# Where three kinds of weight conversions and small loads stand in a two-layer decoder kernel: two slabs in a feature buffer, conversions in the norm chains, loads moved forward

## The chip, the core and the metric

The kernel runs on one core of one Trainium2 chip. The metric is device time in microseconds (us): the median of three runs of the kernel. One further execution was profiled. Its trace records each instruction of the core's engines: TensorE (PE, with its weight loads as PEld), VectorE (DVE), ScalarE (ACT), GpSimd (POOL) and SyncE (SP), which issues almost all of the transfers here. A name such as L235 is line 235 of the kernel before.

## The reference

Two layers over 256 tokens of width 1024, batch 1, all in float32. Each layer is a mixer of three attention groups and then a GeGLU feed-forward network (FFN) with a causal convolution of width 3:

```
for l in range(DEPTH):                       # DEPTH = 2, SEQ = 256, D_MODEL = 1024
    h = rms_norm(x, ln_mix_pre[l])
    x = x + rms_norm(hybrid_mixer(h, rel_bias, w_in[l], b_f[l], q_norm[l], kv_norm[l],
                                  w_uq[l], w_ukv[l], w_o[l]), ln_mix_post[l])
    h = rms_norm(x, ln_ffn_pre[l])
    x = x + rms_norm(conv_ffn(h, w_up[l], conv_w[l], conv_b[l], w_down[l]), ln_ffn_post[l])

def conv_ffn(h, w_up, conv_w, conv_b, w_down):   # D_FF = 2816
    u = h @ w_up                                 # 1024 x 5632
    u = causal_depthwise_conv3(u, conv_w) + conv_b
    g, val = split(u, 2)
    return (gelu(g) * val) @ w_down              # 2816 x 1024
```

The mixer begins with one projection `h @ w_in` (1024 x 2726) and ends with `merged @ w_o` (1024 x 1024). Its columns c (low-rank latents, normed with the gains `q_norm` and `kv_norm`) and v are projected first.

## The kernel before, in words

**Weights come in slabs.** Every weight matrix is read in pieces ("slabs") of up to 128 x 1024 float32. `plan()` lists them in the order of use. For one layer that is c, v, the other columns of `w_in`, o (8 slabs), and then the FFN: slabs gu, g and u of `w_up` and d0 to d21 of `w_down`. In the FFN, d(2i-2) and d(2i-1) follow the up slabs of block i.

**A slab passes through three steps.** `fetch()` issues its load on SP into a `raw` buffer `st` (5 of them, `RBUFS`). `hi_next()` copies it on ACT into a rounded half `wh` (L228). `lo_next()` subtracts that half from the original on DVE and gives `wl` (L235). A product of two float32 matrices is then made from three matmuls (`mm3`, `mm3s`: high by high, high by low, low by high), so PE needs `wh` for the first and `wl` for the second of them. The next fetch into a raw buffer waits for the subtraction that last read it.

**How far ahead a slab is converted.** `slab(key)` is called just before a matmul group. It calls `convert`, which converts up to `AHEAD` = 6 slabs past the one asked for, as long as fewer than `WBUFS` = 8 slabs are converted and not yet used up (`nxt - done < WBUFS`). While `hold` is set, only the slab asked for is made sure of, and the conversions are placed by hand. Each engine runs its instructions in the order in which the program issues them.

**The FFN's loop.** 11 blocks (`NI`) of 256 hidden columns. For i = 2 to 10, `up(i)` makes four accumulations of 128 columns (gate and value), each evicted by ACT (L850) and DVE (L851). `conv_glu(i)` runs the convolution, the gelu and the split on ACT (L863, L876, L275) and DVE (L871, L873, L880, L276). Then `down(i-1, t)` multiplies block i-1 into the accumulators `ac[t]` for the two halves t = 0, 1 of the tokens. The last block runs its two column halves one after the other, each with its own `conv_glu`. For the last four blocks (`SKEW` = 4) the product for t = 1 is put off ("late"). Their d slabs, d14 to d21, so stay in converted buffers until the end. After the loop come `down(7, 1)`, `down(10, 0)`, the post-norm of t = 0 and the pre-norm of t = 0 for the next layer, during which PE runs the late products for t = 1. Then come the same two norms for t = 1, while PE begins the next layer's c and v columns for t = 0.

**The norm chains.** `postnorm` and `prenorm` each take two squares on ACT (L291), a short reciprocal root on POOL (L296 to L298), and two or four DVE operations on 512 columns (L327 and L332, or L312). An argument `mid` is called inside the chain and places conversions there. `to_feat` transposes the normed tokens on PE (L319) and splits them (L275, L276) into a feature pair. A feature pair is one tile `xx` of 128 x 4096 in the pool `xtp`, which has 2 buffers: in the FFN one holds the FFN's input (`fh`, `fl`), the other held the mixer's merged output (`mh`, `ml`).

**The same at the border from mixer to FFN.** The products with `w_o` for t = 1 run while t = 0 is normed, and `up_nat` for t = 0 starts while t = 1 is normed. PE needs slab gu6 for the third step of `up_nat(1, 0)`, then the transposes of t = 1 (in its `mid`), then slab gu7.

**Small loads.** The tile `lc` holds `q_norm`, `kv_norm` and `b_f` of a layer (L605 to L607, 128, 64 and 3 KB). It is first read by the norm of the c columns (L427).

Of the kernel before, what the change touches and what calls it, by code (L numbers as in the profile page):

```python
# [10 lines left out]
F32 = mybir.dt.float32  # L11
F32R = mybir.dt.float32r
# [52 lines left out]
def kernel(ctx: ExitStack, tc: tile.TileContext, x, rel_bias, ln_mix_pre, ln_mix_post,  # L65
# [18 lines left out]
    def acc():  # L84
        return [wk(), wk()]
# [7 lines left out]
    def feat_pair():  # L93
        xx = xtp.tile([128, 8, 2, S], F32R, name="xx")
        return xx[:, :, 0, :], xx[:, :, 1, :]
# [105 lines left out]
    def shaped(t, shp):  # L201
        v = t[:, :int(np.prod(shp))]
        if len(shp) == 3:
            return v.rearrange("p (a g b) -> p a g b", g=shp[1], b=shp[2])
        return v if len(shp) == 1 else v.rearrange("p (a b) -> p a b", b=shp[-1])
# [12 lines left out]

    lows = []

    def hi_next():
        key, (_, shp) = slabs[nxt[0]]
        nxt[0] += 1
        n = int(np.prod(shp))
        st = staged.pop(0)
        h = wpool.tile([128, 1024], F32R, name="wh")
        lo = wpool.tile([128, 1024], F32R, name="wl")
        nc.scalar.activation(h[:, :n], st[:, :n], AF.Copy)  # L228
        lows.append((h, lo, st, n))
        loaded[key] = (shaped(h, shp), shaped(lo, shp))  # L230

    def lo_next():
        if lows:
            h, lo, st, n = lows.pop(0)
            nc.vector.tensor_tensor(lo[:, :n], st[:, :n], h[:, :n].bitcast(F32), op=ALU.subtract)  # L235

    def split_next():
        hi_next()
        lo_next()

    def split_last():
        hi_next()
        lo_next()
# [9 lines left out]
    def slab(key):  # L253
        i = index[key]
        convert(i if hold[0] else i + AHEAD)
        assert key in loaded, key
        left[i] -= 1
        done[0] += left[i] == 0
        return loaded[key]
# [115 lines left out]
    for l in range(L):  # L375
        lc = lay.tile([128, 390], F32, name="lc")
        if l == 0:
            xh, xl = feat_pair()
        else:
            xh, xl = nx  # L380
# [222 lines left out]

        def small_loads():
            nc.sync.dma_start(lc[:, :256], bcast(q_norm[l], 256))  # L605
            nc.sync.dma_start(lc[:, 256:384], bcast(kv_norm[l], 128))
            nc.sync.dma_start(lc[:, 384:390], bcast(b_f[l], 6))  # L607
# [23 lines left out]
        if l == 0:  # L631
# [7 lines left out]
            to_feat(1, hn[1], xh, xl)  # L639
            small_loads()  # L640
            nc.sync.dma_start(cst[:, C_R:], cst_d[:, 256 + C_R:])
# [14 lines left out]
        else:  # L656
            small_loads()
            hold[0] = False
# [136 lines left out]
        hi_next()  # L795
        postnorm(1, wacc[1], g_post, mid=split_last)
        lo_next()
        fetch()
        hn1 = prenorm(1, halves(g_fpre), mid=hi_next)
        lo_next()  # L800
        split_next()
        hold[0] = False
# [104 lines left out]
        for i in range(2, NI):  # L907
# [10 lines left out]
            if i == 2:  # L918
                ac.extend(acc() for _ in range(2))
            if i == 4:  # L920
                g_fpost = gain(ln_ffn_post[l])
# [11 lines left out]
        hold[0] = True  # L933
        postnorm(0, ac[0], g_fpost, out_v[0] if last else None)
        if not last:
            hn_next[0] = prenorm(0, halves(g_pre))
        down(late.pop(0), 1)
        for n in range(2):
            for j in late:
# [4 lines left out]
                down(j, 1, (n,))  # L944
        if not last:
            convert(index[(l + 1, "c", 3)])

        def two():
            fetch()
            if not last:  # L950
                hi_next()
                hi_next()
                lo_next()

        postnorm(1, ac[1], g_fpost, out_v[1] if last else None, mid=two)
        if not last:
            lo_next()
            hn_next[1] = prenorm(1, halves(g_pre), mid=two)
            lo_next()
# [28 lines left out]
```

## Time and profile before

| what | value |
|---|---|
| median of 3 runs | 646.12 us (645.0 to 646.38) |
| the profiled execution, its own time | 644.71 us |
| span of its trace, first to last instruction | 642.8 us |
| PE busy (matmuls) | 621.8 us, 97% of the span |
| PEld busy | 526.7 us, 82% |
| DVE busy | 475.9 us, 74% |
| ACT busy | 402.6 us, 63% |
| POOL busy | 31.7 us, 5% |
| HBM | 107.78 MB read, 169 GB/s over the span |

The table is to be read with the stages in mind: a share over the whole span says little of the few places at which PE stands still. In the rows further down, a time in brackets is how long the engine stood idle before the instruction, with what released it. Matmul ends are modelled, so the distance between two starts is the safer measure of what PE lost.

### The profile page before, as it was taken

The page shows a single profiled execution, that of the slowest core. Times are in us where ns is not written, and L with a number is a line of the kernel's source. Part 1 is how long each engine was busy: PE and PEld are TensorE (multiplying, and loading weights), DVE is VectorE, ACT ScalarE, POOL GpSimd, SP SyncE. Part 2 cuts the span into 40 slices and gives each one's busy share as a digit, 9 for nine tenths or more (in the row PEclk, how much of TensorE's full clock was granted, in tenths as well). Part 3 has the DMA queues.
Part 4 walks back from the last instruction along what each step waited for, and adds up shares of the span by engine and source line. Part 5 has one row for each costly group of instructions (what it writes and reads, how often), then busy time and mean ns, then how long its engine had stood idle before and what let it go on. Part 6 is the DMA issues. An engine that isn't in the chain of part 4 may idle for free.

```text
span 642.8 us, 9945 instructions
## 1 busy us (share of the span) xinstructions
PE 621.8 (97%) x3522; PEld 526.7 (82%) x3522; DVE 475.9 (74%) x963; ACT 402.6 (63%) x801; POOL 31.7 (5%) x74
## 2 busy tenths in 40 slices
PE   7999999999999999999899999999999999999996
PEld 3998988778888888887688988878788888888864
DVE  4683786576888887777777568757588888888873
ACT  5567556656667666665655766566575676666751
POOL 2210000120000000000031000002100000000001
PEclk9999999999999999999999999999999999999999
DMA  7885343346446675553545833433554666566401
GB/s 256 243 278 184 132 154 110 99 157 201 140 140 217 240 252 185 185 184 131 154 140 154 278 132 142 126 94 131 176 184 139 229 228 197 197 196 197 164 1 65
DMA packets 79653, 109.48 MB, mean 170 GB/s; under 512 B 4269, under 2 KB 69523, under 8 KB 79604
## 3 DMA queue, kind: packets, MB, share of 16 engines
q1 hardware_dynamic: 78018, 106.09, 50.5%
q10 hardware_dynamic: 1250, 1.87, 0.8%
q0 software_dynamic: 336, 0.90, 0.5%
q8 instruction: 27, 0.44, 0.3%
q14 instruction: 22, 0.18, 0.1%
HBM read 107.78 MB, written 1.06 MB: 169 GB/s over the span
## 4 chain that ended last, share of the span: by engine, by line
PE 86%; DVE 6%; ACT 3%; issue 2%; POOL 1%; DMA 0%; DVEq 0%; POOLq 0%; ACTq 0%
PE wk L845 19%; PE wk L847 10%; PE wk L262 8%; PE wk L263 8%; PE wk L264 8%; PE wk L269 7%; PE wk L272 7%; PE wk L270 7%; DVE wl L235 2%; PE wk L577 2%; PE wk L585 2%; PE wk L544 1%; PE wk L319 1%; PE wk L542 1%; ACT wh L228 1%
## 5 line engine op out<-in xcount | busy, mean ns | idle before, releaser
L235 DVE TENSOR_TENSOR wl<-st,wh 128x1024 fp32r<-128x1024 f32 (+3 forms) x200 | 230.2, 1184 | 71.1 <-ACT wh L228 70.7
L228 ACT ACTIVATE wh<-st 128x1024 fp32r<-128x1024 f32 (+3 forms) x200 | 196.3, 1022 | 23.0 <-DMA st<-in_w_in_dram 9.1
L845 PE MATMUL wk<-xx,wh 128*128 128x512 f32 x576 | 157.5, 395 | 1.5 <-ACT wh L228 1.5
L845 PEld LDWEIGHTS wk<-xx,wh 128*128 128x128 f32 x576 | 99.6, 189 | 16.1 <-ACT wh L228 1.9
L847 PEld LDWEIGHTS wk<-xx,wl 128*128 128x128 f32 x576 | 88.2, 189 | 12.9 <-DVE wl L235 1.0
L847 PE MATMUL wk<-xx,wl 128*128 128x256 f32 x576 | 91.8, 281 | 0.1
L263 PE MATMUL wk<-wl,hp 128*128 128x512 f32 x176 | 69.5, 395 | 3.0 <-DVE wl L235 3.0
L262 PE MATMUL wk<-wh,hp 128*128 128x512 f32 x176 | 68.9, 391 | 1.1 <-ACT wh L228 1.1
L264 PE MATMUL wk<-wh,hp 128*128 128x512 f32 x176 | 68.9, 392 | 0.0
L270 PE MATMUL wk<-wl,xx 128*128 128x512 f32 (+3 forms) x160 | 58.6, 366 | 3.6 <-DVE wl L235 3.6
L269 PE MATMUL wk<-wh,xx 128*128 128x512 f32 (+3 forms) x160 | 59.5, 372 | 0.6 <-ACT xx L275 0.3
L269 PE MATMUL wk<-xx,wh 128*128 128x256 f32 x192 | 49.5, 291 | 0.0
L270 PE MATMUL wk<-xx,wh 128*128 128x256 f32 x192 | 48.0, 283 | 0.0
L272 PE MATMUL wk<-wh,xx 128*128 128x512 f32 (+3 forms) x160 | 45.1, 363 | 0.9 <-DVE xx L276 0.9
L850 ACT ACTIVATE t<-wk 128x256 f32<-128x256 f32 x72 | 25.9, 372 | 28.8 <-PE wk L847 28.5
L863 ACT ACTIVATE t<-t,cv 128x256 f32<-128x256 f32 x72 | 38.6, 593 | 6.3 <-DVE t L851 6.0
L263 PEld LDWEIGHTS wk<-wl,hp 128*128 128x128 f32 x176 | 33.0, 188 | 11.5 <-DVE wl L235 5.2
L275 ACT ACTIVATE hp<-hv 128x256 fp32r<-128x256 f32 x44 | 18.4, 418 | 35.8 <-DVE hv L880 35.8
L262 PEld LDWEIGHTS wk<-wh,hp 128*128 128x128 f32 x176 | 33.1, 188 | 8.1 <-ACT wh L228 1.6
L264 PEld LDWEIGHTS wk<-wh,hp 128*128 128x128 f32 x176 | 33.1, 188 | 6.8
L269 PEld LDWEIGHTS wk<-xx,wh 128*128 128x128 f32 x192 | 36.7, 191 | 1.7 <-issue 1.3
L851 DVE TENSOR_TENSOR t<-wk,t 128x256 f32<-128x256 f32 x72 | 28.9, 420 | 11.5 <-ACT t L850 11.4
(158 smaller groups left out, 911.3 us busy)
## 6 DMA issues: line engine op xcount, KB each, us to landing
st<-in_w_up_dram SPq DMA_DIRECT2D x72, 512.0 KB, 5.1
st<-in_w_down_dram SPq DMA_DIRECT2D x44, 512.0 KB, 4.7
st<-in_w_in_dram SPq DMA_DIRECT2D x24, 512.0 KB, 4.7
st<-in_w_o_dram SPq DMA_DIRECT2D x16, 512.0 KB, 3.1
st<-in_w_up_dram SPq DMA_DIRECT2D x32, 256.0 KB, 2.9
st<-in_w_in_dram SPq DMA_DIRECT2D x8, 390.0 KB, 7.2
st<-in_w_in_dram SPq DMA_DIRECT2D x8, 384.0 KB, 3.1
st<-in_w_in_dram SPq DMA_DIRECT2D x5, 416.0 KB, 3.3
```

The costliest lines, as they stand in the source:

```text
L228: nc.scalar.activation(h[:, :n], st[:, :n], AF.Copy)
L235: nc.vector.tensor_tensor(lo[:, :n], st[:, :n], h[:, :n].bitcast(F32), op=ALU.subtract)
L262: nc.tensor.matmul(o, stat[0], mov[0], start=start, stop=False)
L263: nc.tensor.matmul(o, stat[0], mov[1], start=False, stop=False)
L264: nc.tensor.matmul(o, stat[1], mov[0], start=False, stop=stop)
L269: nc.tensor.matmul(o, stat[0], mov[0], start=start and i == 0, stop=False)
L270: nc.tensor.matmul(o, stat[0], mov[1], start=False, stop=False)
L272: nc.tensor.matmul(o, stat[1], mov[0], start=False, stop=stop and i == n - 1)
L845: nc.tensor.matmul(ps, wh[:, k % 4, c], both(fh, k), start=k == 0, stop=False)
L847: nc.tensor.matmul(ps[:, :S], wl[:, k % 4, c], fh[:, k, :], start=False, stop=k == 7)
L851: nc.vector.tensor_tensor(us[a][:, g, :], ps[:, :S], us[a][:, g, :], op=ALU.add)
L863: nc.scalar.activation(y[:, g, :], us[a][:, g, :], AF.Identity, scale=cv[:, 88 + cj:89 + cj], bias=cv[:, 132 + cj:133 + cj])
```

## The change

- At block 6 of each FFN, a third tile `ex` is taken from the pool of feature pairs. The converted halves of d14 and d15 (`2 * (NI - SKEW)` is 14) go into it, not into the pool of 8. These two slabs no longer count against `WBUFS`.
- `hi_room()` is a `hi_next()` that runs only where a buffer is free and a slab is left. It stands in both norm chains of t = 0 and in those of t = 1 at the FFN's end.
- The order of conversions at the FFN's end is changed: two to three halves stand in other places among the norms of t = 1, and the slab v3 is converted by the next layer's second `slab` call.
- At the border from mixer to FFN, slab gu6 is converted in the post-norm of t = 1 (its `wl` behind it and ahead of the pre-norm), gu7's `wh` in the pre-norm.
- The loads of `lc` for layer 1 are issued at block 6 of layer 0's FFN, not at the start of layer 1.

```diff
+    extra = {}
+    apart = set()
...
         st = staged.pop(0)
-        h = wpool.tile([128, 1024], F32R, name="wh")
-        lo = wpool.tile([128, 1024], F32R, name="wl")
+        if key in extra:
+            h, lo = extra.pop(key)
+            apart.add(key)
+            done[0] += 1
+        else:
+            h = wpool.tile([128, 1024], F32R, name="wh")
+            lo = wpool.tile([128, 1024], F32R, name="wl")
...
+    def hi_room():
+        if nxt[0] < len(slabs) and nxt[0] - done[0] < WBUFS:
+            hi_next()
...
-        done[0] += left[i] == 0
+        done[0] += left[i] == 0 and key not in apart
...
         else:
-            small_loads()
             hold[0] = False
...
-        postnorm(1, wacc[1], g_post, mid=split_last)
+
+        def three():
+            hi_next()
+            lo_next()
+            hi_next()
+
+        postnorm(1, wacc[1], g_post, mid=three)
+        lo_next()
         lo_next()
         fetch()
         hn1 = prenorm(1, halves(g_fpre), mid=hi_next)
         lo_next()
-        split_next()
         hold[0] = False
...
+            if i == 6:
+                ex = xtp.tile([128, 8, 2, S], F32R, name="xx").rearrange("p a b c -> p (a b c)")
+                for j in range(2):
+                    extra[(l, "d", 2 * (NI - SKEW) + j)] = [ex[:, 2048 * j + 1024 * n:2048 * j + 1024 * n + 1024]
+                                                            for n in range(2)]
+                if not last:
+                    lc = lay.tile([128, 390], F32, name="lc")
+                    small_loads(l + 1)
...
         hold[0] = True
-        postnorm(0, ac[0], g_fpost, out_v[0] if last else None)
+        fetch()
+        postnorm(0, ac[0], g_fpost, out_v[0] if last else None, mid=hi_room)
+        lo_next()
         if not last:
-            hn_next[0] = prenorm(0, halves(g_pre))
+            hn_next[0] = prenorm(0, halves(g_pre), mid=hi_room)
+            lo_next()
         down(late.pop(0), 1)
...
-        if not last:
-            convert(index[(l + 1, "c", 3)])
+        fetch()
+        hi_room()
+        lo_next()
+        hi_room()
 
         def two():
+            lo_next()
             fetch()
-            if not last:
-                hi_next()
-                hi_next()
-                lo_next()
+            hi_room()
+            hi_room()
 
         postnorm(1, ac[1], g_fpost, out_v[1] if last else None, mid=two)
         if not last:
             lo_next()
-            hn_next[1] = prenorm(1, halves(g_pre), mid=two)
+            lo_next()
+            hn_next[1] = prenorm(1, halves(g_pre), mid=hi_room)
             lo_next()
```

## Rows read from the trace of the kernel before

**Rows 1.** The page, part 1: busy us, share, instructions.

```profile
PE 621.8 (97%) x3522; PEld 526.7 (82%) x3522; DVE 475.9 (74%) x963; ACT 402.6 (63%) x801; POOL 31.7 (5%) x74
```

**Rows 2.** Windows: stretch, its length, busy us (instructions) by engine, granted clock, DMA.

```profile
125.00:150.00 25.00, 24.02 (x114) 19.58 (x113) 18.42 (x24) 15.42 (x26) 4.92 (x11) 1.00 0.47 151
...
278.23:292.20 13.97, 13.97 (x78) 12.07 (x77) 12.27 (x22) 9.69 (x18) 0.00 (x0) 1.00 0.48 162
...
325.00:345.00 20.00, 17.71 (x95) 15.81 (x94) 15.36 (x25) 12.16 (x26) 5.51 (x12) 1.00 0.54 153
...
638.00:640.00 2.00, 0.00 (x0) 0.00 (x0) 1.46 (x3) 0.00 (x0) 0.27 (x1) 1.00 0.03 11
640.00:642.80 2.80, 0.00 (x0) 0.00 (x0) 0.00 (x0) 0.00 (x0) 0.00 (x0) 0.74 0.48 179
```

**Rows 3.** Timeline of PE, mixer to FFN: start, us, instruction, [idle before <-releaser].

```profile
140.92 0.39 PE L269 MATMUL wk<-wh,xx 128*128 128x512 f32 x1
142.28 0.50 PE L270 MATMUL wk<-wl,xx 128*128 128x512 f32 x1 [0.98 <-DVE wl L235]
142.62 0.40 PE L269 MATMUL wk<-wh,xx 128*128 128x512 f32 x1
```

**Rows 4.** Timeline of PE, end of layer 0's FFN and start of layer 1.

```profile
295.90 0.64 PE L847 MATMUL wk<-xx,wl 128*128 128x256 f32 x4
297.31 1.21 PE L845 MATMUL wk<-xx,wh 128*128 128x512 f32 x4 [0.77 <-ACT wh L228]
...
313.52 0.49 PE L262 MATMUL wk<-wh,hp 128*128 128x512 f32 x1 [1.15 <-ACT wh L228]
...
315.12 0.39 PE L264 MATMUL wk<-wh,hp 128*128 128x512 f32 x1
...
323.53 1.03 PE L319 MATMUL wk<-ident,scr 128*128 128x128 f32 x8
...
339.69 0.64 PE L272 MATMUL wk<-wh,xx 128*128 128x416 f32 x2 [0.92 <-DVE xx L276]
```

**Rows 5.** Timeline of PE, end of layer 1's FFN.

```profile
610.18 1.19 PE L845 MATMUL wk<-xx,wh 128*128 128x512 f32 x4 [0.77 <-ACT wh L228]
...
626.58 0.40 PE L264 MATMUL wk<-wh,hp 128*128 128x512 f32 x1
```

**Rows 6.** Timeline of DVE, end of layer 0's FFN and start of layer 1.

```profile
283.33 2.36 DVE L235 TENSOR_TENSOR wl<-st,wh 128x1024 fp32r<-128x1024 f32 x2 [0.53 <-ACT wh L228]
...
290.54 0.48 DVE L871 SCALAR_TENSOR_TENSOR t<-t,cv,t 128x255 f32<-128x255 f32 x1
...
300.25 0.48 DVE L871 SCALAR_TENSOR_TENSOR t<-t,cv,t 128x255 f32<-128x255 f32 x1
...
307.88 0.42 DVE L851 TENSOR_TENSOR t<-wk,t 128x256 f32<-128x256 f32 x1
...
321.99 1.42 DVE L312 SCALAR_TENSOR_TENSOR scr<-x,r,gain 128x512 f32<-128x512 f32 x2 [1.91 <-POOL r L298]
...
338.95 1.28 DVE L276 TENSOR_TENSOR xx<-wk,xx 128x512 fp32r<-128x512 f32 x2
```

**Rows 7.** Timeline of ACT, end of layer 0's FFN.

```profile
295.89 0.42 ACT L275 ACTIVATE hp<-hv 128x256 fp32r<-128x256 f32 x1 [0.83 <-DVE hv L880]
...
303.06 1.04 ACT L228 ACTIVATE wh<-st 128x1024 fp32r<-128x1024 f32 x1
...
310.69 0.42 ACT L275 ACTIVATE hp<-hv 128x256 fp32r<-128x256 f32 x1 [0.96 <-DVE hv L880]
...
312.42 2.63 ACT L228 ACTIVATE wh<-st 128x1024 fp32r<-128x1024 f32 x3
```

**Rows 8.** Timeline of SP's queue (issues), and landing of slabs from 245 to 300 us.

```profile
284.58 0.37 SPq L216 DMA_DIRECT2D st<-in_w_up_dram  x1
...
332.74 0.46 SPq L605 DMA_DIRECT2D lc<-in_q_norm_dram  x1
...
DMA to landing us min/median/max: 3.3/5.1/5.6
```

More of the change, by code (lines that the diff above doesn't have):

```diff
@@ L237, in split_next @@
     def split_next():
-        hi_next()
-        lo_next()
-    def split_last():
         hi_next()
@@ L375 @@
     for l in range(L):
-        lc = lay.tile([128, 390], F32, name="lc")
         if l == 0:
+            lc = lay.tile([128, 390], F32, name="lc")
             xh, xl = feat_pair()
@@ L601, in heads, with small_loads @@
                                          [vtile("c", t, h) for t in range(2)], r))
-        def small_loads():
+        def small_loads(l):
             nc.sync.dma_start(lc[:, :256], bcast(q_norm[l], 256))
@@ L639 @@
             to_feat(1, hn[1], xh, xl)
-            small_loads()
+            small_loads(0)
             nc.sync.dma_start(cst[:, C_R:], cst_d[:, 256 + C_R:])
@@ L656 @@
         else:
-            small_loads()
             hold[0] = False
@@ L919 @@
                 ac.extend(acc() for _ in range(2))
+            if i == 6:
[4 more added lines that the diff above has]
+                if not last:
+                    lc = lay.tile([128, 390], F32, name="lc")
+                    small_loads(l + 1)
             if i == 4:
@@ L944 @@
                 down(j, 1, (n,))
-        if not last:
-            convert(index[(l + 1, "c", 3)])
+        fetch()
+        hi_room()
+        lo_next()
+        hi_room()
         def two():
+            lo_next()
             fetch()
-            if not last:
-                hi_next()
-                hi_next()
-                lo_next()
+            hi_room()
+            hi_room()
         postnorm(1, ac[1], g_fpost, out_v[1] if last else None, mid=two)
```

## The prediction, made before the changed kernel ran

> **What bounds the kernel now.** I read the shares of the page first. PE is busy 97% of the span [rows 1], so the change can only win back what PE loses in its gaps, some 20 us, of which the start and the last norm chain are not touched. The windows come next, to see where the gaps lie: 1.0 us between mixer and FFN and 2.3 us around the start of layer 1 [rows 2], and, by PE's timeline, the end of each FFN [rows 4, 5]. There the reader is to look at starts. A matmul of 512 columns follows the one before after 0.2275 us, a group of eight in `up` takes 1.40 us.
>
> - Mixer to FFN, once in each layer: from 140.92 to 142.62 PE starts two matmuls in 1.70 us, where 0.455 is regular. PE loses 1.24 us to the `wl` of gu6 (0.98 idle, the rest is the filling of the pipeline) [rows 3].
> - End of layer 0's FFN: the group after 295.90 should start 0.47 later, at 296.37, and starts at 297.31. From there to 315.12 lie five groups of `up` (7.0 us) and 29 matmuls (6.6), and it takes 17.81 [rows 4]. Lost: 0.94 + 4.21 = 5.15 us, to the `wh` and `wl` of u21, d18, d19 and d21, all of them conversions that came late.
> - End of layer 1's FFN: the same 13.6 us of work takes 626.58 - 610.18 = 16.40, so 2.8 + 0.94 = 3.7 us [rows 5]. It is less because no table load and no slab of a next layer stand there.
>
> **Why these conversions come late.** In blocks 7 to 9 the late d slabs stay in the pool of 8, so `convert` finds no room and issues u21 behind `conv_glu(9)`, d18 to d20 in block 10, and d21 behind `conv_glu(10)` and the table load. I counted `nxt - done` by hand through both programs. With d14 and d15 apart, the two lost places return: g20 to u21 are issued in the first six groups of `up(9)`, d18 and d19 behind `conv_glu(9)`, d20, d21 and c0 in block 10, c1 behind the table load. No conversion is then late for PE. These edits add no instruction, and the tile they use was last read by the products with `w_o`.
>
> **The queues, and what is late next.** ACT and DVE run in order, and a conversion issued earlier stands ahead of other work. In `up(9)` DVE is already busy 12.27 of 13.97 us [rows 2], since a block without its t = 1 product is shorter for PE and not for DVE. So I follow DVE from 283.33, where both programs are still alike. Two conversions take 2.36 us [rows 6], so they start 1.14 apart; an eviction (L851, 0.42) is taken as 0.34 apart.
>
> 1. DVE now has six conversions (d16, d17, g20, g21, u20, u21) and four evictions ahead of the convolution of block 9: 283.35 + 6 x 1.14 + 4 x 0.34 = 291.55. Before, it began at 290.54 [rows 6]. Lag 1.0.
> 2. The last `hp` of block 9 moves from 295.89 [rows 7] to 296.9. Then d18's `wh` runs to 298.3, DVE subtracts d18 and d19 to 300.6, and only then comes the eviction that the first half of block 10 waits for. Its scaling on ACT (0.6) follows, and the convolution starts at 301.8. Before: 300.25 [rows 6]. Lag 1.5.
> 3. d20's `wh` takes the place that d18's had at 303.06 [rows 7], 1.5 later. DVE has the same number of entries as before up to the last eviction, three conversions and one eviction, but one of the three is c0, 832 columns wide, estimated from its width at 0.24 less. The last eviction moves from 307.88 [rows 6] to 309.1, `hp` of the last half block from 310.69 [rows 7] to 311.95, done at 312.4.
>
> PE reaches `down(10, 0)`, second half block, at 315.12 - 0.455 - 5.15 = 309.5. It waits for `hp` until 312.4 and restarts for 0.1. The new wait costs 3.0 us where five old ones cost 5.15: **2.1 us** are left. In layer 1 neither c0 nor c1 exists, so the last eviction is not behind c0 (0.9): the wait is 2.0 + 0.1, and 3.7 - 2.1 = **1.6 us** are left.
>
> By the Trainium skill ("Perfetto Trace Analysis", Optimization Strategy), a gap that repeats on the engine that should be full can mean that there are too few buffers for the next tile. By that reading two more slabs' worth of buffers takes all of these waits, and the sum would be 5.15 + 3.7 + 2.5 = 11.3; by the rows on DVE's queue it is 6.2. No run yet tells which.
>
> **Uncertain in this part.** u21's load is issued at 284.58, since it waits for d16's subtraction in both programs. Landing takes 3.3 to 5.6 us [rows 8]. ACT could use it at 287.5; DVE gets to u21 at 289.7, so a landing of up to 4.1 us costs nothing, and 5.6 costs 1.5 us in each layer. I take nothing, as the transfers are busy only 0.48 of that stretch [rows 2]. Towards the other side, if `conv_glu` moved along with PE, the wait would be some 0.5 us in layer 0 and none in layer 1.
>
> **Norms of t = 0 at the FFN's end.** `hi_room` issues nothing there: in layer 0 d16 to d21, c0 and c1 fill the 8 places, in layer 1 no slab is left. The chain itself now follows a single conversion (c1), not three [rows 7]. Its normed first half was ready 0.8 us before PE's transposes (321.99 + 0.75 against 323.53) [rows 4, 6]. I work the chain out as up to 0.6 later against PE, so 0 is lost; without that cover 0.6 would be.
>
> **Norms of t = 1 and start of layer 1.** The `wl` of c3, v0 to v2 move behind the post-norm's and pre-norm's operations, v3 behind `slab(c1)`. DVE's set of work between the split of t = 0 and that of t = 1 is unchanged: six conversions, six norm operations, the c-norm. The split that PE waits for last (338.95, PE at 339.69) [rows 4, 6] comes at the end of this set in both orders. The waits ahead of it shift (c3, v0 and v2 would be late by 0.7, 1.0 and 1.1 us by my sum, v1 and v3 no longer), and their total stays. I take **0**. Bounds: a gain of the last wait (0.92 + 0.27 = 1.2) and a loss of one conversion (1.0).
>
> **Mixer to FFN.** gu6's `wh` goes right behind gu5's, on an ACT that then waits for the chain. DVE subtracts it in the 1 us in which it stood before L312 for POOL, so gu6 is ready ahead of the pre-norm and not behind it, 1.3 us earlier. L312 then ends 0.1 later, over 1 us ahead of the transposes. PE's 1.24 us go, in both layers: **2.5 us**. If the pre-norm slipped by more than that 1 us, the wait would move to the transposes.
>
> **Small loads.** Three issues of some 0.45 us leave SP's queue at 332.74 [rows 8], where no slab load behind them was late for PE, and go to block 6, where SP stands waiting for a raw buffer. 195 KB at the 162 GB/s of such a block [rows 2] are 1.2 us of transfer, the most that they can delay a slab. I take 0.
>
> **The sum.** 2.1 + 1.6 + 2.5 + 0 = 6.2 us. The profiled execution took 644.71 us (span 642.8 and 1.9 around it) and would take 638.5. The median of the runs is 1.4 above it: 646.12 - 6.2 = 639.9.
>
> **Rivals.**
>
> - *DVE keeps up.* The convolution of block 10 moves with PE, and the waits go almost whole: 2.5 + 4.7 + 3.7 = 10.9, so 635.2. For it: DVE still has idle time in that stretch; against it: the six conversions of step 1 come in one piece. This is how the skill's rule on repeating gaps, named above, would have it.
> - *The lag grows.* Late landing of u21, or dependencies that I did not see on the shared tile, add 1 to 1.8 us per layer: 642 to 643.5. If the lag takes everything at the FFN's ends, only 2.5 are left, 643.6.
> - *The change does nothing there and elsewhere.* It needs 3.1 us more lag per layer than I worked out: 646.
> - *Slower, by PE's clock.* The new single wait (2.9 us) is longer than any of those before (1.15) [rows 4]. At the span's end PE does nothing from 638 to 640 at a granted clock of 1.00, and then the mean falls to 0.74, so the granted clock does go from 2.4 towards 1.2 GHz after idling [rows 2]. If it falls here, each us at 1.2 GHz loses half of itself. From 12.4 us at the low level in both layers together the gain is gone; with 8 us behind each wait it is 646.12 - 6.2 + 8 = 647.9. Against it: that idle stretch began before 638 and the clock held through 640. The Trainium skill ("TensorE: Matmul & The Clock Gate", Part 1) has the low clock as the state that idling brings back; the fall at the span's end agrees with it.
>
> **How the numbers follow.** Forecast as worked out 0.60 (its own range 638.5 to 641.5), DVE keeps up 0.13, lag grows 0.14, nothing 0.07, slower 0.06. The first three are faster by over 0.2% (1.3 us, about what a measurement of this kernel tells from no change): 0.87, same 0.07, slower 0.06. The range takes in the first three cases: 635.0 to 643.7.
>
> **What would show it.** Right: no wait for `wh` or `wl` in PE's timeline at the FFN's ends, in their place one wait of L262 for `hp` (L275), about 2.9 us in layer 0 and 2.0 in layer 1; no wait for gu6 in either layer; the start of layer 1 as long as before. Wrong: that wait under 1 us (DVE kept up) or over 4 (lag), a granted clock under 1.00 behind it, or a new wait at the transposes of t = 0 or t = 1.

## The result, and the profile after

The changed kernel took **641.23 us** (median of 5 executions, 639.1 to 642.71) against 646.12, a ratio of 0.9921 [0.9901, 0.9941]. The forecast was 639.9. The profiled execution took 639.1 us; its span is 637.3 us against 642.8, so 5.5 us less where the sum had 6.2. Line numbers shift: L228 is now L235 (`wh`), L235 is L246 (`wl`), L262 to L264 are L269 to L271, L269, L270 and L272 are L276, L277 and L279, L275 and L276 are L282 and L283, L319 is L326, L850 and L851 are L862 and L863, L863 is L875, L871 is L883, L880 is L892. In the kernels of the experiments they shift again, so there go by the tiles.

The page's first part, to be held against [rows 1]:

```profile
PE 618.4 (97%) x3522; PEld 526.7 (83%) x3522; DVE 475.3 (75%) x963; ACT 402.7 (63%) x801; POOL 33.6 (5%) x74
```

Each of these engines runs as many instructions as before. What changed is when PE stands still. The window around the border from mixer to FFN, as in [rows 2]:

```profile
125.00:150.00 25.00, 25.00 (x119) 20.76 (x119) 19.63 (x24) 15.41 (x26) 5.92 (x11) 1.00 0.50 154
```

PE is busy 25.00 of 25.00 us where it was 24.02, and the wait of [rows 3] is gone (in layer 1 too, where the like window of 35 us is full). PE's timeline at the end of layer 0's FFN and the start of layer 1, for [rows 4], and at the end of layer 1's FFN, for [rows 5]:

```profile
308.15 0.39 PE L271 MATMUL wk<-wh,hp 128*128 128x512 f32 x1
311.92 0.50 PE L269 MATMUL wk<-wh,hp 128*128 128x512 f32 x1 [3.38 <-ACT hp L282]
312.26 0.40 PE L270 MATMUL wk<-wl,hp 128*128 128x512 f32 x1
...
320.89 1.03 PE L326 MATMUL wk<-ident,scr 128*128 128x128 f32 x8
327.19 0.46 PE L277 MATMUL wk<-wl,xx 128*128 128x416 f32 x1 [0.29 <-DVE wl L246]
329.39 0.44 PE L277 MATMUL wk<-wl,xx 128*128 128x384 f32 x1 [0.80 <-DVE wl L246]
333.25 0.45 PE L277 MATMUL wk<-wl,xx 128*128 128x384 f32 x1 [1.51 <-DVE wl L246]
337.35 0.65 PE L279 MATMUL wk<-wh,xx 128*128 128x416 f32 x2 [0.27 <-DVE xx L283]
...
618.57 0.39 PE L271 MATMUL wk<-wh,hp 128*128 128x512 f32 x1
620.58 0.50 PE L269 MATMUL wk<-wh,hp 128*128 128x512 f32 x1 [1.62 <-ACT hp L282]
620.92 0.40 PE L270 MATMUL wk<-wl,hp 128*128 128x512 f32 x1
```

The timeline lists no wait for a weight at either FFN's end. One wait for the last `hp` stands in their place. Between starts, layer 0 loses 311.92 - 308.15 - 0.23, and 0.11 of filling: 3.65 us where it lost 5.15. Layer 1 loses 1.89 where it lost 3.7. From the transposes of t = 0 to the last wait for the split, the start of layer 1 takes 337.35 - 320.89 = 16.46 us against 16.16. So the span's 5.5 us are 1.5 + 1.8 + 2.5 - 0.3.

ACT, DVE and SP at the end of layer 0's FFN, in this order, for [rows 6 to 8]:

```profile
288.20 1.06 ACT L235 ACTIVATE wh<-st 128x1024 fp32r<-128x1024 f32 x1 [1.75 <-DMA st<-in_w_up_dram]
...
311.45 0.42 ACT L282 ACTIVATE hp<-hv 128x256 fp32r<-128x256 f32 x1 [0.97 <-DVE hv L892]
...
287.35 1.22 DVE L246 TENSOR_TENSOR wl<-st,wh 128x1024 fp32r<-128x1024 f32 x1
289.29 1.23 DVE L246 TENSOR_TENSOR wl<-st,wh 128x1024 fp32r<-128x1024 f32 x1 [0.72 <-ACT wh L235]
...
301.22 0.48 DVE L883 SCALAR_TENSOR_TENSOR t<-t,cv,t 128x255 f32<-128x255 f32 x1 [0.34 <-ACT t L875]
...
283.39 0.37 SPq L216 DMA_DIRECT2D st<-in_w_up_dram  x1
```

The row at 288.20 is the one to read. ACT stood idle for the landing of u21, issued at 283.39, so some 4.8 us earlier. DVE, which had just done u20, then stood idle 0.72 us for ACT, with everything of steps 1 to 3 queued behind. Against the rows of before, less the 1.2 us that the border won, the convolution of block 10 starts 301.22 - 300.25 + 1.2 = 2.2 later (worked out: 1.5) and the split of the last `hp` 311.45 - 310.69 + 1.2 = 2.0 later (1.3). Both are 0.7 more than worked out.

### The profile page after: what moved, and what is told of

It reads as the page before. It is cut to its first block, busy times and chain, and to the rows that moved or that the text cites. A ratio compares the mean times of both kernels' runs of the same rounds, so it can differ in the third digit from the quotient of the medians.

```text
span 637.3 us, 9937 instructions
## 1 busy us (share of the span) xinstructions
PE 618.4 (97%) x3522; PEld 526.7 (83%) x3522; DVE 475.3 (75%) x963; ACT 402.7 (63%) x801; POOL 33.6 (5%) x74
## 4 chain that ended last, share of the span: by engine, by line
PE 82%; DVE 8%; ACT 4%; DMA 2%; issue 2%; POOL 0%; DVEq 0%; POOLq 0%; ACTq 0%
PE wk L857 16%; PE wk L276 8%; PE wk L859 8%; PE wk L279 8%; PE wk L277 8%; PE wk L269 8%; PE wk L270 8%; PE wk L271 8%; DVE wl L246 3%; PE wk L584 2%; DVE t L885 2%; DVE t L883 2%; PE wk L592 2%; ACT wh L235 1%; PE wk L551 1%
## 5 line engine op out<-in xcount | busy, mean ns | idle before, releaser
L246 DVE TENSOR_TENSOR wl<-st,wh 128x1024 fp32r<-128x1024 f32 (+3 forms) x196 | 225.1, 1182 | 68.4 <-ACT wh L235 66.0
L235 ACT ACTIVATE wh<-st 128x1024 fp32r<-128x1024 f32 (+3 forms) x196 | 192.2, 1021 | 23.5 <-DMA st<-in_w_up_dram 10.4
L857 PEld LDWEIGHTS wk<-xx,wh 128*128 128x128 f32 x576 | 99.6, 189 | 14.2
L269 PE MATMUL wk<-wh,hp 128*128 128x512 f32 x160 | 62.7, 392 | 5.0 <-ACT hp L282 5.0
L271 PE MATMUL wk<-wh,hp 128*128 128x512 f32 x160 | 62.6, 391 | 0.0
L270 PE MATMUL wk<-wl,hp 128*128 128x512 f32 x160 | 62.6, 391 | 0.0
L277 PE MATMUL wk<-wl,xx 128*128 128x512 f32 (+3 forms) x160 | 58.2, 364 | 3.2 <-DVE wl L246 3.2
L276 PE MATMUL wk<-wh,xx 128*128 128x512 f32 (+3 forms) x160 | 59.3, 370 | 0.5 <-ACT wh L235 0.5
L276 PE MATMUL wk<-xx,wh 128*128 128x256 f32 x192 | 49.5, 290 | 0.0
L277 PE MATMUL wk<-xx,wh 128*128 128x256 f32 x192 | 48.0, 282 | 0.0
L279 PE MATMUL wk<-wh,xx 128*128 128x512 f32 (+3 forms) x160 | 45.1, 363 | 0.3 <-DVE xx L283 0.3
L875 ACT ACTIVATE t<-t,cv 128x256 f32<-128x256 f32 x72 | 38.6, 593 | 9.5 <-DVE t L863 9.1
L282 ACT ACTIVATE hp<-hv 128x256 fp32r<-128x256 f32 x44 | 18.4, 418 | 35.8 <-DVE hv L892 35.8
L862 ACT ACTIVATE t<-wk 128x256 f32<-128x256 f32 x72 | 25.4, 372 | 23.4 <-PE wk L859 23.4
L269 PEld LDWEIGHTS wk<-wh,hp 128*128 128x128 f32 x160 | 30.1, 188 | 11.5 <-ACT hp L282 5.8
L276 PEld LDWEIGHTS wk<-xx,wh 128*128 128x128 f32 x192 | 36.6, 191 | 1.7 <-issue 1.3
L303 POOL TENSOR_TENSOR r<-ms,epsb 128x1 f32<-128x1 f32 x16 | 8.0, 500 | 563.5 <-ACT junk L298 563.5
L888 ACT ACTIVATE ge<-t 128x256 f32<-128x256 f32 x44 | 18.2, 414 | 30.2 <-DVE t L885 30.2
L277 PEld LDWEIGHTS wk<-xx,wh 128*128 128x128 f32 x192 | 36.7, 191 | 0.1
```

The lines of the kernel that those rows point to most:

```text
L269: nc.tensor.matmul(o, stat[0], mov[0], start=start, stop=False)
L270: nc.tensor.matmul(o, stat[0], mov[1], start=False, stop=False)
L271: nc.tensor.matmul(o, stat[1], mov[0], start=False, stop=stop)
L276: nc.tensor.matmul(o, stat[0], mov[0], start=start and i == 0, stop=False)
L277: nc.tensor.matmul(o, stat[0], mov[1], start=False, stop=False)
L279: nc.tensor.matmul(o, stat[1], mov[0], start=False, stop=stop and i == n - 1)
```

## Experiments

All were timed in five rounds beside the kernel before, except the last, which was run once.

### The two parts alone

**Third tile only**: the kernel before with d14 and d15 in the feature tile, nothing else.

```diff
+        if key in extra:
+            h, lo = extra.pop(key)
+            apart.add(key)
+            done[0] += 1
...
+                for j in range(2):
+                    extra[(l, "d", 2 * (NI - SKEW) + j)] = [ex[:, 2048 * j + 1024 * n:2048 * j + 1024 * n + 1024]
+                                                            for n in range(2)]
```

> The kernel before with one part of the change: d14 and d15 in the feature buffer. No order of norms, no border from mixer to FFN, no small loads changed. Theory (parts add up as in the trace of the changed kernel): at equal clock (executions at 0.998 or more) 1.5 us are won at the end of layer 0's FFN and 1.8 in layer 1, so a span of about 639.5; PE keeps the 1.0 us waits for gu6 and shows single waits for hp of 3.4 and 1.6 us. The 3.4 us wait lets the clock fall in some executions as in the changed kernel, so the median gains less, 1 to 3 us. Rival (the slabs give all that the change gave): span about 637.3.

Measured: 644.14 us, ratio 0.9968 [0.9947, 0.9989], profiled span 639.7 at a mean granted clock of 0.999. DVE's wait for u21, the new wait of PE, and the border's wait, from its timelines:

```profile
290.21 1.23 DVE L242 TENSOR_TENSOR wl<-st,wh 128x1024 fp32r<-128x1024 f32 x1 [0.24 <-ACT wh L235]
...
312.83 0.50 PE L269 MATMUL wk<-wh,hp 128*128 128x512 f32 x1 [2.90 <-ACT hp L282]
...
142.50 0.50 PE L277 MATMUL wk<-wl,xx 128*128 128x512 f32 x1 [1.01 <-DVE wl L242]
```

The tile alone makes the new wait, and leaves the border's. This time u21 landed earlier: DVE stood idle 0.24 us, not 0.72, and the wait is 2.90, not 3.38 (3.4 was expected). Both differ by 0.48. The start of layer 1 shows one wait more, for the small loads, which stand at their old place here:

```profile
335.05 0.48 DVE L434 SCALAR_TENSOR_TENSOR t<-wk,r,lc 128x256 f32<-128x256 f32 x1 [0.52 <-DMA lc<-in_q_norm_dram]
```

**Everything but the third tile.**

```diff
-                ex = xtp.tile([128, 8, 2, S], F32R, name="xx").rearrange("p a b c -> p (a b c)")
-                for j in range(2):
-                    extra[(l, "d", 2 * (NI - SKEW) + j)] = [ex[:, 2048 * j + 1024 * n:2048 * j + 1024 * n + 1024]
-                                                            for n in range(2)]
```

> The changed kernel without the third feature tile: d14 and d15 stay in the pool of 8. Theory: the five waits for wh and wl at the FFN's ends come back (3.45 us idle in layer 0), no wait for hp; 2.5 us are won at the two borders from mixer to FFN and 0.3 lost at the start of layer 1, so a span of about 640.6 at equal clock. No wait at the FFN's end is over 1.2 us, so the clock falls there in no execution, only at the kernel's start as in the kernel before. Rival (the slabs give all): span as before, 642.8.

Measured: 644.3 us, ratio 0.9956 [0.9936, 0.9976]. The execution of the shortest span has 640.5 us. The profiled one has 642.5, the old waits at the FFN's end (1.13 and 0.76 the last of them), and behind them this (windows: stretch, length, busy us by engine, granted clock, DMA):

```profile
312.00:314.00 2.00, 0.60 (x2) 0.28 (x2) 1.38 (x2) 2.00 (x3) 0.00 (x0) 1.00 0.00 0
314.00:316.00 2.00, 2.00 (x6) 1.55 (x7) 2.00 (x3) 0.85 (x3) 0.19 (x1) 0.55 0.52 100
316.00:318.00 2.00, 2.00 (x7) 1.62 (x6) 0.41 (x1) 0.44 (x1) 0.00 (x0) 0.60 0.95 314
```

By the shortest spans of the executions (642.6 before, 640.5 here, 639.7 with the tile only, 637.1 changed) this part wins 2.1 us and the tile 2.9, together 5.0 of 5.5. Where the other 0.5 comes from isn't shown; landings alone differ by as much from one execution to the next (0.24 against 0.72 for u21). And the granted clock fell behind waits that the kernel before has too, where no fall was expected.

### What sets the length of the new wait

**Longer queue**: two more DVE operations of 128 x 1024 ahead of the last convolution of each layer. Their results are used by nothing.

```diff
                     up(i, us, ((0, a), (1, a)))
+                    if a == 1:
+                        for _ in range(2):
+                            nc.vector.tensor_tensor(scr(), g_fpost, g_fpost, op=ALU.mult)
```

> The changed kernel with two further DVE operations of 128x1024 (result used by nothing) between the last evictions of the last half block and its convolution, in each layer. Theory of the queue: hp comes later by their length, 2 x 1.1 to 1.2 us, and both waits grow by it, to some 5.7 and 3.9 us; the time grows by 4.6 us at equal clock. Rival (ACT or a transfer sets hp, DVE has room): the waits grow by less than 1 us each. For the clock: with longer waits the theory of the clock expects it to fall oftener, and the time to grow by more than 4.6 us in most executions.

Measured: 648.73 us, ratio 1.0022 [1.0002, 1.0041], profiled span 649.5 at 0.982. PE's two waits:

```profile
316.89 0.79 PE L269 MATMUL wk<-wh,hp 128*128 128x512 f32 x1 [5.74 <-ACT hp L282]
...
630.10 0.79 PE L269 MATMUL wk<-wh,hp 128*128 128x512 f32 x1 [3.90 <-ACT hp L282]
```

Each wait grew by what was put in front of it (2.36 and 2.28), as expected, so DVE's queue sets it: nothing between DVE and PE has slack here. The median rose by 7.4 us, the waits by 4.6; the mean clock of its executions is 0.982 to 0.992, against 0.990 to 0.998 without the two operations.

**Less in the queue**: c0 and c1 are held back to the norms of t = 0 (`cap` is the last d slab during block 10).

```diff
-        convert(i if hold[0] else i + AHEAD)
+        convert(i if hold[0] else min(i + AHEAD, cap[0]))
...
+            if i == NI - 1:
+                cap[0] = index[(l, "d", NJ - 1)]
```

> The changed kernel with one limit: in the last block no slab past d21 is converted, so c0 and c1 wait until the norms of t = 0, where hi_room now finds room and converts them. Theory of the queue: c0's subtraction (0.9 us) leaves DVE's queue ahead of the last eviction, hp of layer 0 comes 0.9 us earlier, and the wait falls from 3.4 to about 2.5; layer 1 stays at 1.6, where no slab c exists. At equal clock 0.9 us are won, if c0 and c1 find idle time in the norms; the clock falls less often. Rival (ACT's conversions, not DVE's, delay hp): c0's wh on ACT ran while ACT waited for the eviction anyway, and the wait falls by less than 0.3.

Measured: 639.16 us, ratio 0.9895 [0.9868, 0.9922], profiled span 636.9. DVE's wait for u21, then PE's wait:

```profile
289.82 1.22 DVE L247 TENSOR_TENSOR wl<-st,wh 128x1024 fp32r<-128x1024 f32 x1 [0.94 <-ACT wh L236]
...
311.51 0.50 PE L270 MATMUL wk<-wh,hp 128*128 128x512 f32 x1 [2.66 <-ACT hp L283]
```

The wait fell by 0.72 although u21 came 0.22 later for DVE than in the changed kernel, so c0 in the queue cost 0.94. The rival's less than 0.3 is excluded.

**PE arrives later**: the last block's products take both column halves of its first half block, then those of the second, for which PE waits.

```diff
-        down(NI - 1, 0)
+        for a in range(2):
+            for n in range(2):
+                c = slice(n * 512, n * 512 + 512)
...
+                mm3(ac[0][n], (hs[NI - 1][a][0][:, tok(0)], hs[NI - 1][a][1][:, tok(0)]), (wh[:, c], wl[:, c]),
+                    False, j == NJ - 1)
```

> The changed kernel with the products of the last block in another order: both column halves of the accumulator for the first half block, then both for the second. PE has three more matmuls (0.68 us) to do ahead of the one that waits for hp. Theory of the queue (the wait ends when hp is ready, whatever PE does): the waits fall from 3.4 to 2.7 and from 1.6 to 0.9 us, hp keeps its time, and 1.4 us are won at equal clock. Rival (the wait is for something that moves with PE): the waits stay as they are, no gain.

Measured: 639.81 us, ratio 0.9878 [0.9852, 0.9905], profiled span 636.4. DVE's wait for u21, then PE's:

```profile
289.22 1.23 DVE L246 TENSOR_TENSOR wl<-st,wh 128x1024 fp32r<-128x1024 f32 x1 [0.92 <-ACT wh L235]
...
311.85 0.50 PE L269 MATMUL wk<-wh,hp 128*128 128x512 f32 x1 [2.90 <-ACT hp L282]
320.51 1.29 PE L326 MATMUL wk<-ident,scr 128*128 128x128 f32 x8 [0.21 <-DVE scr L319]
...
620.37 0.50 PE L269 MATMUL wk<-wh,hp 128*128 128x512 f32 x1 [0.95 <-ACT hp L282]
```

Both waits are shorter by 0.68, once the later u21 (0.92 against 0.72) is taken off. The span won 0.9, where 1.4 was expected: 0.2 went to u21, and 0.21 came back at the transposes, which now reach the norm of t = 0 too early.

**The changed kernel again**, unchanged.

> The changed kernel once more, to see how its executions spread. Its five executions so far took 639.1 to 642.7 us at mean granted clocks of 0.998 to 0.991, where the one of the kernel before with a listed clock had 0.999. Theory of the clock: PE's new single wait of 3.4 us (layer 0) lets the granted clock fall in some executions, so a lower mean clock goes with a longer span (about 3 us for 0.006), and the kernel before stays at 0.998 or more in all of its own. Rival: the spread is in the measurement, and spans do not follow the clocks or the kernel before spreads as well.

Measured: 641.35 us, ratio 0.9909 [0.9879, 0.9938]. Its profiled execution has a span of 640.7 at a mean clock of 0.991, u21 late by 0.68 for DVE, and a wait of 3.34. The expectation is half right. A lower mean clock does go with a longer span, but the kernel before doesn't stay at 0.998: its 17 executions beside this run took 644.55 to 650.01 us at mean clocks of 0.999 to 0.991. Taken at equal clock, 0.998 or more, the spans of the kernel before are 642.6 to 643.6 us in all rounds of these experiments, and those of the changed one 637.1 and 637.3.

**Old order of the conversions in the norms of t = 1**, the rest as changed.

```diff
-        fetch()
-        hi_room()
-        lo_next()
-        hi_room()
+        if not last:
+            convert(index[(l + 1, "c", 3)])
...
-            hn_next[1] = prenorm(1, halves(g_pre), mid=hi_room)
+            hn_next[1] = prenorm(1, halves(g_pre), mid=two)
```

> The changed kernel with the order of before in the norms of t = 1 at the FFN's end. Theory (DVE's set of work between the two splits sets the end of this stretch, not its order): PE's waits move back to v1, v2 and v3, and the stretch from the first c product to the last wait for xl differs by at most 0.3 us from the 14.2 us of the changed kernel (13.9 before). Rival (the new order of conversions wins or costs over 1 us there): 13.2 or less, or the changed kernel's loss comes from there, with 1 us won.

Measured: 640.91 us, ratio 0.9913 [0.989, 0.9935], profiled span 638.6 at 0.997, u21 late by 0.97 for DVE, a wait of 3.62. The stretch from the transposes to the last wait for the split is 338.62 - 322.61 = 16.01 against 16.46. The difference of 0.45 is more than the 0.3 that the theory allowed and less than the 1 us of the rival. Since the clock fell at 312 to 318 us and PE came later to the stretch, a second run with the old order follows below.

**The law.** In all these runs the wait in layer 0 is 2.66 us, plus what DVE stood idle for u21, less 0.94 where c0 and c1 are held back, less 0.68 (three matmuls of 0.2275) where PE takes the first half block's products first:

| run | DVE idle for u21 | wait by the law | measured |
|---|---|---|---|
| third tile only | 0.24 | 2.90 | 2.90 |
| changed, again | 0.68 | 3.34 | 3.34 |
| changed | 0.72 | 3.38 | 3.38 |
| old order, t = 1 | 0.97 | 3.63 | 3.62 |
| c0, c1 held back | 0.94 | 2.66 | 2.66 |
| other order of products | 0.92 | 2.90 | 2.90 |
| both (below) | 0.59 | 1.63 | 1.63 |

The 2.66 and the 0.94 are taken from these rows; the others test them. What DVE stood idle follows in turn from the landing of u21, counted from its issue on SP to the start of its copy on ACT. It is the landing less 4.1 us, the free bound of the prediction: 4.31 us gave 0.24, 4.81 gave 0.72, 5.06 gave 0.97. Layer 1's wait is 1.62 to 1.64 in all of them that leave it alone: there u21 lands after 3.4 to 3.6 us, and DVE loses nothing.

### Both edits, and the granted clock

**Both edits together.**

> Both shortenings of the new wait together: c0 and c1 are held back to the norms of t = 0, and the last block's products take both column halves of its first half block before the second. Queue theory (the wait is the distance between PE's arrival and the split of the last hp, and the two edits act on its two ends): the wait of layer 0 goes from 2.66 by 6 matmuls less (0.68) to 2.0, give or take 0.25 for the landing of u21; layer 1 to 0.95. Span about 635.7 at a granted clock of 0.998, median about 638. Rival (another dependency of the last half block holds both): the wait stays at 2.6 and the span at 636.9, median 639.2.

Measured: 638.06 us (636.98 to 640.47), ratio 0.9881 [0.9861, 0.9901], profiled span 636.4 at 0.995, shortest 635.2. DVE's wait, then PE's:

```profile
290.35 1.23 DVE L247 TENSOR_TENSOR wl<-st,wh 128x1024 fp32r<-128x1024 f32 x1 [0.59 <-ACT wh L236]
...
312.05 0.50 PE L270 MATMUL wk<-wh,hp 128*128 128x512 f32 x1 [1.63 <-ACT hp L283]
```

The two add up; 2.0 was expected for the 0.94 of u21, and it was late by 0.59. The rival's 2.6 is excluded.

**The wait filled**: the changed kernel with 13 matmuls in layer 0's wait and 6 in layer 1's, whose results nothing uses.

```diff
+        fps = wk()
+        nf = 6 if last else 13
+        for q in range(nf):
+            nc.tensor.matmul(fps, hs[NI - 2][0][0][:, tok(0)], loaded[(l, "d", NJ - 3)][0][:, :512],
+                             start=q == 0, stop=q == nf - 1)
         down(NI - 1, 0)
```

> The changed kernel with 13 further matmuls of 512 columns (layer 1: 6) right ahead of the products of the last block, where PE stands waiting; their result is used by nothing. They take 13 x 0.2275 = 3.0 us of a wait of 3.4, and 1.4 us of 1.6, so the work itself ends at the same time. Theory of the clock: PE no longer idles there, the clock stays at 0.998 in all executions, and the median falls to the level of the fastest execution of the changed kernel, about 639 us. Rival (the clock has nothing to do with the spread): median and spread as in the changed kernel, about 641 us, or a little above it.

Measured: 638.88 us (638.4 to 641.76), ratio 0.9881 [0.9853, 0.991], the waits 0.58 and 0.28. The median came down to the expected level, but the interval overlaps that of the changed kernel, and the clock didn't stay at 0.998 in all executions: two of six have 0.994 and 0.992. To be held against it, the profiled execution of the changed kernel's second run, by windows:

```profile
310.00:312.00 2.00, 0.00 (x0) 0.00 (x0) 1.82 (x5) 0.88 (x2) 0.00 (x0) 0.89 0.85 239
312.00:314.00 2.00, 1.31 (x3) 1.12 (x4) 0.61 (x2) 1.75 (x3) 0.00 (x0) 0.50 0.44 161
314.00:316.00 2.00, 2.00 (x6) 1.52 (x6) 1.12 (x2) 1.42 (x3) 0.45 (x1) 0.50 0.03 8
316.00:318.00 2.00, 2.00 (x7) 1.52 (x6) 0.79 (x2) 0.69 (x2) 0.18 (x1) 0.50 0.40 87
318.00:320.00 2.00, 2.00 (x9) 1.62 (x8) 1.73 (x3) 0.48 (x1) 0.56 (x2) 0.90 0.29 110
```

and that with the wait filled:

```profile
10.00:20.00 10.00, 7.72 (x33) 6.21 (x33) 6.95 (x10) 6.36 (x12) 2.30 (x5) 0.83 0.71 215
...
308.00:312.00 4.00, 4.00 (x19) 3.32 (x18) 3.93 (x8) 2.36 (x5) 0.00 (x0) 1.00 0.60 151
312.00:316.00 4.00, 3.42 (x15) 2.42 (x14) 1.63 (x4) 3.01 (x6) 0.00 (x0) 1.00 0.44 157
```

After the wait of 3.34 us, PE came back at a granted clock of 0.50, which is the level of 1.2 GHz, and 2.4 GHz (1.00) was back by 320 us. With the wait filled the clock stays at 1.00 there in this execution. It is low at 10 to 20 us, where the other execution too has 0.83. But in its first execution the changed kernel held 1.00 with the wait unfilled. So neither that the filling keeps the clock up nor that the spread of the executions comes from this wait is shown.

**Both edits, and 7 and 3 such matmuls in what is left of the waits.**

> The kernel with both shortenings, with 7 (layer 0) and 3 (layer 1) matmuls of 512 columns ahead of what is left of the wait, whose result nothing uses. Theory of the clock (it falls behind the idle stretch in part of the executions, and a TensorE that works through it doesn't fall): waits of 0.4 and 0.3, the best execution as without the filling (span 635.7), no execution with a fall at 310 to 320 us, median 0.5 to 1 below that without. Rival (the spread of the executions has nothing to do with these waits): same median and spread as without the filling.

Measured: 636.91 us (636.42 to 637.46), ratio 0.9859 [0.984, 0.9878], profiled span 634.6 at 0.999. It beats both kernels. No execution lies above 637.46, where without the filling two of six lay above 638.9; but the intervals of the two ratios overlap. Two more things speak against putting all of this down to the filling. The profiled execution without it has its fall at 10 to 20 us (0.83) and none behind its wait. And with the filling u21 landed after 4.03 us, so DVE lost nothing to it and layer 0 shows no wait at all (0.4 was expected): part of the way from 636.4 to 634.6 is this landing.

**The same with the old order in the norms of t = 1.**

> The kernel with both shortenings and the filling, with the order of the kernel before in the norms of t = 1. If the new order there costs the 0.3 to 0.45 us that the stretch from the transposes of t = 0 to the last wait for the split shows (16.46 against 16.01 in the run with the old order), the span falls by 0.4 to 635.3 and the median with it. Rival (that stretch only gave back what the other edits had won before it, since DVE ends it in both): no change of the span.

Measured: 636.52 us, ratio 0.9857 [0.9838, 0.9876], profiled span 634.6. The span is the same, as the rival has it, but not for the rival's reason. DVE between the split of t = 0 and that of t = 1, in the run with the new order and then in that with the old one:

```profile
320.15 1.29 DVE L284 TENSOR_TENSOR xx<-wk,xx 128x512 fp32r<-128x512 f32 x2 [0.40 <-ACT xx L283]
322.79 1.41 DVE L335 TENSOR_TENSOR scr<-wk,gain 128x512 f32<-128x512 f32 x2 [0.34 <-ACT junk L299]
328.91 1.42 DVE L320 SCALAR_TENSOR_TENSOR scr<-x,r,gain 128x512 f32<-128x512 f32 x2 [0.71 <-POOL r L306]
334.61 1.28 DVE L284 TENSOR_TENSOR xx<-wk,xx 128x512 fp32r<-128x512 f32 x2
```

```profile
320.56 1.29 DVE L284 TENSOR_TENSOR xx<-wk,xx 128x512 fp32r<-128x512 f32 x2 [0.40 <-ACT xx L283]
328.86 0.96 DVE L247 TENSOR_TENSOR wl<-st,wh 128x768 fp32r<-128x768 f32 x1 [0.81 <-ACT wh L236]
334.57 1.28 DVE L284 TENSOR_TENSOR xx<-wk,xx 128x512 fp32r<-128x512 f32 x2
```

The last split ahead of PE came at the same time in both. But the execution with the old order was 0.40 us later already when it issued u21's load (283.88 against 283.48), where the two programs don't differ yet, and PE's transposes of t = 0 began at 319.30 in it against 318.89. From there to the last wait for the split it took 16.01 us, as in the earlier run with the old order, and the one with the new order 16.46. DVE does the same operations. With the new order it stands idle 0.34 and 0.71 us among them, with the old one 0.81. So the new order makes this stretch 0.45 us longer; 0.24 of it are these waits, the rest lies in breaks too short for the timeline to list. Whether the old one shortens the median isn't shown: 636.52 against 636.91 lies within the noise.

**The kernel before, one look.**

> The kernel before, once more, for its granted clock by windows. If a fall of the clock needs one long idle stretch of TensorE, this kernel shows none at 310 to 320 us, where its waits are 0.3 to 1.2 us each; if a run of short waits is enough, as in the run without the third tile (0.55 to 0.60 behind 1.13 and 0.76), some of its executions show one there. Falls at the kernel's start can be in either.

Measured: 651.27 us, span 649.5 at a mean clock of 0.987, with the same waits for weights as in [rows 4] (1.13 and 0.76 the last two). By windows:

```profile
10.00:20.00 10.00, 7.67 (x28) 6.22 (x29) 7.24 (x10) 6.73 (x13) 2.30 (x5) 0.73 0.74 220
...
318.00:320.00 2.00, 2.00 (x7) 1.60 (x6) 1.81 (x3) 0.69 (x2) 0.28 (x1) 0.59 0.67 184
320.00:322.00 2.00, 2.00 (x6) 1.54 (x6) 0.69 (x1) 0.69 (x2) 0.65 (x2) 0.56 0.96 308
```

So the kernel before loses its clock in the same two places: at its start, and at the FFN's end behind two waits of about a microsecond. Its start of layer 1 also shows that the small loads could be late where they stood. DVE's first operation with `lc`, with the subtraction ahead of it where nothing is listed between: in this execution, in the first one of the kernel before, and in the run with the old order and moved loads:

```profile
341.50 0.48 DVE L427 SCALAR_TENSOR_TENSOR t<-wk,r,lc 128x256 f32<-128x256 f32 x1 [1.04 <-DMA lc<-in_q_norm_dram]
...
335.30 0.95 DVE L235 TENSOR_TENSOR wl<-st,wh 128x768 fp32r<-128x768 f32 x1
336.32 0.48 DVE L427 SCALAR_TENSOR_TENSOR t<-wk,r,lc 128x256 f32<-128x256 f32 x1
...
334.38 0.95 DVE L246 TENSOR_TENSOR wl<-st,wh 128x768 fp32r<-128x768 f32 x1
335.25 0.47 DVE L434 SCALAR_TENSOR_TENSOR t<-wk,r,lc 128x256 f32<-128x256 f32 x1
```

With the 1.04 us of waiting, it is 344.88 - 327.74 = 17.14 us here from the transposes of t = 0 to the last wait for the split, where the others take 16.16 and 16.01.

## Why the prediction was right, and where it was off

- **Mixer to FFN**, 2.5 us: right. No wait there in either layer, and the run without the tile keeps this gain.
- **Which wait takes the place of the old ones**: right. It is the one for `hp`, in both layers, and DVE's queue sets it: put 2.3 us in front and it grows by that, take c0 and c1 out and it shrinks by 0.94 (the prediction priced c0 there at 0.9).
- **Its size in layer 0**, 3.0 us: measured 3.65. The step that failed is "I take nothing" for the landing of u21. The bound stood there, free up to 4.1 us, and so did the median landing of 5.1 [rows 8], which lies above it; "nothing" went by the low share of busy transfers instead. The landing took 4.8, and DVE lost the 0.72 between. Without it the idle time would be 2.66, where 2.9 was worked out. The like landing in the third-tile run cost 0.24. What makes the landing long, and lets it change from 4.0 to 5.1 us between runs, stays open; an earlier load of u21 wasn't tried.
- **In layer 1**, 2.1 us: measured 1.89, so the end of layer 1 gave 1.8 us where 1.6 was worked out.
- **Start of layer 1**, 0 with bounds of -1.2 and +1.0: measured 0.3 more. The waits named there (c3, v0, v2) are the three that the trace shows. That the total of the waits stays is what failed: this took DVE's work for the length of the stretch and left out what DVE stands idle in it, which is more with the new order. The stretch takes 16.45 to 16.75 us in the nine runs that have it, 16.01 in the two with the old order and moved loads. The 0.45 show as only 0.3 because the kernel before took 16.16.
- **Small loads and norms of t = 0**, 0: no row shows a loss; the transposes of t = 0 (320.89) have no wait. The moved loads win something that the prediction didn't look for, since it asked which slabs they delay and not when `lc` itself lands. In the kernel before, DVE's first operation with `lc` starts 336.32 - 335.30 = 1.02 us after the subtraction ahead of it; in the run with the old order and moved loads that is 0.87. The 0.15 between is just what 16.16 has over 16.01. No wait is listed there, so that it is for `lc` is inferred, from the listed waits of 0.52 and 1.04 in two other runs with the loads at their old place. Two misses of opposite sign, 0.45 and 0.15, so make the 0.3, and that it is small is in part luck.
- **From span to median.** By the times of the profiled executions the change won 644.71 - 639.1 = 5.6 us, so the sum was off by 0.6 (0.7 by the spans). Another 0.7 lies in the reference point: the median before is 1.4 above its profiled execution, that after 2.1 above its own. Together they are the 1.3 us between 639.9 and 641.23.
- **Rivals.** "DVE keeps up" is excluded by the 3.38 us. The Trainium skill's rule on repeating gaps ("Perfetto Trace Analysis", Optimization Strategy) says that they can come of too few buffers. The trace agrees, since the waits for weights went with the room; but DVE's order put one of 3.38 us in their place, so they didn't go whole. "The lag grows" came about in part, by the cause that it names (u21's landing), and stayed below its 1 us. "Slower, by PE's clock" had its mechanism right and its premise wrong. The clock does fall behind the new wait in some executions (0.50 from 312 to 318 us), which the prediction named as a sign of being wrong, but [rows 4] show waits of at most 1.15 us, and behind such waits the kernel before falls as well. So a fall of the clock isn't peculiar to the changed kernel, and a low mean clock goes with a long span in both. How often each kernel falls there isn't shown, with two profiled executions of each.

## What to carry to other kernels

Room for more converted weights removes the waits for weights, but in-order engines then do those conversions earlier, ahead of what PE needs next: write down the queue of the engine that converts, and price the first item behind the new ones. The wait that results can be shortened at both ends, by holding back conversions that nobody needs yet (0.94 us here) and by giving PE all the work that doesn't need the late operand first (0.68 us). Where a step's cost turns on a landing time close to its free bound, put the overrun into the sum (0.7 us here), not only into the range. And where an order of work is changed on an engine that sets the end of a stretch, count its idle time in both orders (1.05 against 0.81 us here), not only its operations.

## What the runs showed of the hardware that was not expected

- The granted clock depends on the execution, not only on the program. The same changed kernel waits 3.38 us at 1.00 in one execution and falls to 0.50 behind 3.34 us in another; the kernel before holds 1.00 through 1.15 and 0.76 us in one and falls to 0.59 and 0.56 behind 1.13 and 0.76 in another. The Trainium skill ("TensorE: Matmul & The Clock Gate", Part 1) says that the number of slow matmuls at a kernel's start varies from run to run of one kernel. The rows of the start agree (1.00 at 10 to 20 us in the first execution of the changed kernel, 0.83 in the second).
- Two falls (at 10 to 20 us and at 312 to 320) go with a span of the changed kernel's second run that is 3.4 us longer than that of its first, 640.7 against 637.3. Of these, 0.8 are there by the wait's end (312.69 against 311.92) and 3.4 by the transposes of t = 0 (324.32 against 320.89).
- The kernel's start (10 to 20 us) falls to 0.73 or 0.83 in some executions of several of these kernels, and no edit here touches it.
